# Two-layer encoder on one core: the first weights of the second MLP are made on ACT and POOL while the attention's out-projection still runs, with sums in place and eight operands in borrowed buffers

## The chip, the cores and the metric

One core of a Trainium2 chip. TensorE (PE) multiplies matrices, VectorE (DVE), ScalarE (ACT) and GpSimd (POOL) do elementwise work, SyncE (SP) issues nearly all DMAs. Each engine takes its instructions in the order of its own queue, and semaphores hold an instruction until what it needs is done. The metric is the device time of one execution in microseconds; lower is better. "The clock" is the TensorE clock that the profile says was granted, as a share of full speed.

## The reference

Two residual layers on 1024 tokens of width 1024 (8 tiles of 128 tokens), each a token mixer and a gated MLP. Layer 0 mixes by pooling, layer 1 by differential attention. What matters here is the end of the attention and the MLP behind it:

```python
def _diff_attention(...):
    ...
    return o.reshape(b, s, h * 2 * dh) @ w_o

def _conv_ffn(x, w_up, conv_w, conv_b, w_down):
    g, u = jnp.split(x @ w_up, 2, axis=-1)
    ...                       # gc = conv_b + three-tap convolution of g along the tokens
    act = jax.nn.gelu(gc.astype(jnp.float32), approximate=False).astype(x.dtype)
    return (act * u) @ w_down

# in reference(), per layer i
        h = h + y
        h = h + _conv_ffn(_rms_norm(h, ffn_norm[i]), ffn_w_up[i], ffn_conv_w[i], ffn_conv_b[i], ffn_w_down[i])
```

## The kernel before

**Numbers in two parts.** A float32 operand is held as hi + lo, two fp32r tiles: ACT copies the source into hi (a CAST), and DVE or POOL subtracts hi from the source into lo. A product is three matmuls, hi·hi, hi·lo, lo·hi.

**The MLP's up-projection** runs in 22 units j of 128 columns of u and 128 of g. A unit is a 2 by 2 block product done with seven products instead of eight: its weights are four blocks u1, u2, g1, g2 (512 contraction rows each) and three running sums of them; the tokens are seven activation operands x[1] to x[7], made once for all units. Each product is 12 matmuls of 512 columns, so a unit is 84 matmuls. `load` (L382) fetches a unit's two 512 KB raw weight tiles ru and rg, `prep` (L397) makes its seven operand pairs with `parts` (L391: cast on ACT, subtraction on POOL or DVE), `unit` (L499) issues the products in the order 1, 6, 2, 7, 5, 4, 3. Pairs are in the pool `wc`, which has 16 buffers; `prep` of unit 0 of a layer makes its sums into tiles of the pool `s` and does all but two of its subtractions on DVE (L404).

**The stretch around the change** is the entry to the second MLP. The four last head pairs of the out-projection matrix take all 16 buffers of `wc` (`wo_l`, L1385). `wo_rest` (L1394) runs over the token tiles in the order 0, 4, 1, 5, 2, 6, 3, 7: 24 matmuls into two accumulators `wo_acc`; then `add_halves` (L171) adds the residual on DVE and squares on ACT, `rstd` (L179) makes the scale `rn_v`, and `norm_to_x` (L301) scales the tile into `xs` on ACT (L306), transposes it on PE into `tp` (L313, eight transposes) and reads that out (L323 on DVE, L345 on ACT). `each_with_lag` (L366) emits a tile's `combine` after the next tile's first part: for tiles 0 to 3 it only splits the two halves (x[1] and x[2], in `hnT_hi` and `hnT_lo` of half 0); for tiles 4 to 7 it makes the four sums of the block scheme with the partner tile (L354, L355, L356 and L358, all DVE, SBUF operands) and splits x[3] and x[5] (`hnT` of half 1) and x[4], x[6], x[7] (`x_hi`, `x_lo`), with lo on DVE for two and on POOL for three (L318, L319). After the third tile (`early`, L1405) the MLP generator is started: it emits `load(0)` and, of `prep(0)`, the pairs for products 1 and 2 and the first two sums with the pair for product 6. The rest comes after `load(1)` at the end of the stretch (L731).

The queues of this stretch are ordered by a scheduler from the order of emission, priorities and its own costs; from unit 1 on, PE, DVE and ACT keep the order of emission (L736). Pools `cm` and `wd` have one buffer each, of 8 KB per partition, and no compute instruction touches them through unit 0: `w_combos` of unit 1 (L450) loads 1 MB into `wd` on SP, which is issued at 1286 us, among the loads at the start of the out-projection, and lies there until four DVE sums at L456 to L462 take it from 1463.68 us; `cm` is used from unit 2 by `m_combos` (L467). The functions below have the line numbers of the profile.

Of the kernel before, what the change touches and what calls it, by code (L numbers as in the profile page):

```python
# [12 lines left out]
F32R = mybir.dt.float32r  # L13
I32 = mybir.dt.int32
AF = mybir.ActivationFunctionType
ALU = mybir.AluOpType
# [4 lines left out]
P = 128  # L21
# [3 lines left out]
NF = DFF // P  # L25
NT = S // P
NK = D // P
ORDER = (0, 4, 1, 5, 2, 6, 3, 7)
PLAN = ("...saq.bS..c.p", "st.aS.m.q.fb....F.c..")
PLAN7 = (".as.b....S.pqc.", "tmsaSqcb..f......F..")  # L30
# [59 lines left out]
def trunk_kernel(  # L90
# [36 lines left out]
    def f32(ap):  # L127
        return ap.bitcast(F32)
# [18 lines left out]

    hnT = [[hp.tile([P, NK, 512], F32R, name=f"hnT_{n}{hf}") for n in ("hi", "lo")] for hf in range(2)]
    h_dram = [[dram.tile([P, D], F32, name=f"h_dram{i}_{t}") for t in range(NT)] for i in range(4)]
# [82 lines left out]

    gcol = cp.tile([P, 4, NK], F32, name="gcol")
    neglam = cp.tile([P, 1], F32, name="neglam")
# [66 lines left out]
    def norm_to_x(layer, tt, ar, h_t, ss):  # L301
# [19 lines left out]
        def gained(q, dst):  # L321
            gk = gcol[:, 2 + layer, 4 * q:4 * q + 4].unsqueeze(2).broadcast_to([P, 4, P])
            V.tensor_tensor(dst, pts[q], gk, ALU.mult)  # L323
            return dst

        q0, q1 = slice(0, 4), slice(4, 8)
        if tt < 4:
            xf = ar.xf[tt] = ar.tile("raw", [P, NK, P], F32, "xf")
            gained(0, xf[:, q0])
# [36 lines left out]
    def each_with_lag(tiles, first, early=None):  # L366
        late = None
        for tt in tiles:
            nxt = first(tt)
            if late is not None:  # L370
                late()
            late = nxt
            if tt == 1 and early is not None:
                early()
        late()

    def ffn(layer, ar, tail, extra=None):
        G = nc.gpsimd
        wup, wdn, cv = w_up[layer], w_down[layer], convp[layer]
        raws, ws = {}, {}  # L380

        def load(j):  # L382
            if j >= NF:
                return
            raws.setdefault(j, [])
            for off in (DFF, 0):
                r = ar.tile("g" if layer == j == 0 else "raw", [P, NK, P], F32, "raw")
                nc.sync.dma_start(r, wup[:, off + j * P:off + (j + 1) * P].rearrange("(k p) f -> p k f", p=P))
                raws[j].append(r)

        def parts(src, eng=G):  # L391
            hi, lo = (ar.tile("wc", [P, 4, P], F32R, n) for n in ("w_hi", "w_lo"))
            A.copy(hi, src)  # L393
            eng.tensor_tensor(lo, src, f32(hi), ALU.subtract)  # L394
            return hi, lo

        def prep(j):  # L397
            if j >= NF:
                return
            w = ws.setdefault(j, {})  # L400
            ru, rg = raws.pop(j)
            u1, u2, g1, g2 = ru[:, 0:4], ru[:, 4:8], rg[:, 0:4], rg[:, 4:8]

            eng = (V, G)[j > 0]  # L404

            def s_tile(a, b, op):
                t = ar.tile("s", [P, 2, 512], F32, "s")[:, 0].rearrange("p (k f) -> p k f", f=P)
                eng.tensor_tensor(t, a, b, op)  # L408
                return t

            w[1] = parts(u1, G)
            if j == 0:
                w[2] = parts(u2, G)
            yield
            s1 = s_tile(g1, g2, ALU.add)
            s2 = s_tile(s1, u1, ALU.subtract)
            w[6] = parts(s2, eng)
            yield
            if j:
                w[2] = parts(u2)  # L420
            yield
            w[7] = parts(s_tile(u1, g1, ALU.subtract), eng)
            yield
            w[5] = parts(s1, eng)
            yield
            w[4] = parts(g2, eng)
            yield
            w[3] = parts(s_tile(u2, s2, ALU.subtract), eng)
            yield
# [293 lines left out]
            return ends[2:]  # L723

        load(0)
        first = prep(0)
        next(first)
        if layer:
            next(first)
        yield  # L730
        load(1)  # L731
        for _ in first:
# [17 lines left out]
    ar = Arena("a")  # L750
# [123 lines left out]
    def tail0(tt, r):  # L874
        return norm_to_hnT(ar.h[tt], tt, ar, r)

    mlp = ffn(0, ar, tail0, lambda: before_attention())
    pool_band(0)

# [149 lines left out]
    def proj_qk(j, hf):  # L1029
# [5 lines left out]
        for h in range(2):  # L1035
            acc = ps_pj.tile([P, 512], F32, name="pj")
            n = 0
            for k in range(NK):
                whi, wlo = w_qk[j][k // 2]
                for l, r in ((whi, xhi), (wlo, xhi), (whi, xlo)):  # L1040
                    PE.matmul(acc, l[:, k % 2, h], r[:, k], start=(n == 0), stop=(n == 3 * NK - 1))  # L1041
                    n += 1
# [201 lines left out]
    ar = Arena("b")  # L1244
# [83 lines left out]
    with tc.manual_schedule(engines={mybir.EngineType.PE}):  # L1328
        for g in range(H * NT + 2):
            j, i = divmod(g, NT)  # L1330
# [53 lines left out]
    for j in range(4, 8):  # L1384
        hi, lo = ([ar.tile("wc", [P, 512], F32R, "wo_l") for _ in range(2)] for _ in range(2))  # L1385
        r = ar.tile("raw", [P, D], F32, "rawo")
        nc.sync.dma_start(r, w_o[0][j * P:(j + 1) * P, :])
        for n in range(2):
            A.mul(hi[n], halves(r)[n], subsc)
            V.scalar_tensor_tensor(lo[n], halves(r)[n], subsc, f32(hi[n]), ALU.mult, ALU.subtract)  # L1390
        grp.append((j, hi, lo))
    mlp = ffn(1, ar, lambda *a: tail1(*a), lambda: final_gain())

    def wo_rest(tt):  # L1394
# [9 lines left out]

    each_with_lag(ORDER, wo_rest, lambda: next(mlp))  # L1405

# [55 lines left out]
```

## Time and profile before

| | us |
|---|---|
| three timed runs: median (lowest to highest) | 2075.48 (2073.23 to 2075.9) |
| the profiled execution's own time | 2074.96 |
| its span in the trace | 2073.2 |
| so outside the span | 1.76 |
| mean granted TensorE clock | 0.986 |

The profile's page gives busy time by engine and the chain that ended last; the view of windows gives the same for a stretch, with its granted clock; the view of waits says who waited for whom; the timeline lists instructions with start and duration in us and, in brackets, the idle time ahead of one and what ended it. The stretch of the change is 1360 to 1460 us of the span.

### The profile page before, as it was taken

Reading aid. Unit: us, or ns where it says so; the run is one execution under the profiler, and the core shown is the slowest. Engines: PE = TensorE matmul, PEld = TensorE weight load, DVE = VectorE, ACT = ScalarE, POOL = GpSimd, SP = SyncE. Lnnn points to the kernel's source line nnn. Section 1 sums busy time; section 2 is a strip of 40 time slices with the busy share of each in tenths; the row PEclk is TensorE's granted clock in tenths of the full one; section 3 lists DMA queues with packets and bytes.
Section 4 is the critical chain, followed back from the end, with each engine's and each line's share of the span. In section 5 each row is a group of like instructions: output and inputs, shape, how many; then the busy total and the mean of one; then the engine's idle time right before and its main releaser. Section 6 shows DMA issues by size and latency. Waiting matters only on the chain.

```text
span 2073.2 us, 27646 instructions
## 1 busy us (share of the span) xinstructions
PE 1999.2 (96%) x9659; PEld 1664.9 (80%) x9659; DVE 1553.3 (75%) x2286; ACT 1023.5 (49%) x1838; POOL 891.7 (43%) x676
## 2 busy tenths in 40 slices
PE   6799999999999999999999998998999999999998
PEld 6678888888888877888888887876888888888886
DVE  7867777777675658999889987767766777775665
ACT  7733333333453646666667666565433333344343
POOL 4499999996000000101110111115999999930000
PEclk9899999999999999999999999998999999999999
DMA  4325464453976522122212115253445445458663
GB/s 172 104 90 174 138 192 143 157 173 128 378 227 209 193 67 67 43 70 65 64 44 75 56 42 188 102 191 114 128 142 192 148 158 175 140 197 334 200 212 133
DMA packets 221720, 301.90 MB, mean 146 GB/s; under 512 B 17852, under 2 KB 142092, under 8 KB 218764
## 3 DMA queue, kind: packets, MB, share of 16 engines
q1 hardware_dynamic: 221580, 300.13, 44.4%
q8 instruction: 76, 1.25, 0.3%
q14 instruction: 64, 0.52, 0.1%
HBM read 196.78 MB, written 90.70 MB: 139 GB/s over the span
## 4 chain that ended last, share of the span: by engine, by line
PE 87%; DVE 6%; ACT 2%; DMA 2%; issue 1%; SPq 1%; DVEq 0%; ACTq 0%
PE dn L610 19%; PE up_b L436 17%; PE up_c L436 11%; PE up_a L436 11%; PE pj L1041 7%; PE sc L1127 5%; PE pj L1083 4%; PE po L1169 3%; PE aT L1158 3%; PE pj L1265 2%; PE pp L862 1%; DVE nm L1129 1%; PE pl L842 1%; PE wo_acc L1265 1%; DMA kf<-t 1%
## 5 line engine op out<-in xcount | busy, mean ns | idle before, releaser
L1109 POOL TENSOR_TENSOR q_lo<-qt,q_hi 128x256 fp32r<-128x256 f32 x64 | 49.6, 776 | 680.5 <-ACT q_hi L1108 626.7
L394 POOL TENSOR_TENSOR w_lo<-s,w_hi 128x512 fp32r<-128x512 f32 x168 | 270.6, 1610 | 19.4 <-ACT w_hi L393 19.1
L610 PE MATMUL dn<-hnT_hi 128*128 128x512 f32 x560 | 218.1, 389 | 0.0
L610 PE MATMUL dn<-hnT_hi,hnT_lo 128*128 128x512 f32 x560 | 217.9, 389 | 0.0
L610 PE MATMUL dn<-hnT_lo,hnT_hi 128*128 128x512 f32 x560 | 217.9, 389 | 0.0
L436 PE MATMUL up_b<-x_hi,w_hi 128*128 128x512 f32 x528 | 207.2, 393 | 5.2 <-ACT x_hi L318 4.4
L436 PE MATMUL up_b<-x_lo,w_hi 128*128 128x512 f32 x528 | 207.2, 392 | 1.7 <-DVE x_lo L319 1.7
L394 POOL TENSOR_TENSOR w_lo<-raw,w_hi 128x512 fp32r<-128x512 f32 x130 | 193.7, 1491 | 30.8 <-ACT w_hi L393 29.6
L436 PE MATMUL up_b<-x_hi,w_lo 128*128 128x512 f32 x528 | 206.5, 391 | 0.0
L393 ACT CAST w_hi<-s 128x512 fp32r<-128x512 f32 x176 | 108.7, 618 | 178.7 <-PE up_b L436 90.0
L1129 DVE TENSOR_REDUCE nm<-sc 128x1 f32<-128x1024 f32 x128 | 155.8, 1217 | 15.1 <-PE sc L1127 14.7
L593 ACT CAST hnT_hi<-mst 128x1024 fp32r<-128x1024 f32 (+1 forms) x76 | 74.7, 983 | 167.2 <-PE dn L610 127.5
L594 DVE TENSOR_TENSOR hnT_lo<-mst,hnT_hi 128x1024 fp32r<-128x1024 f32 (+1 forms) x76 | 86.5, 1138 | 92.0 <-ACT hnT_hi L593 91.9
L1132 ACT ACTIVATE prob<-sc,nm 128x1024 f32<-128x1024 f32 x128 | 142.7, 1115 | 23.8 <-DVE nm L1129 11.4
L436 PE MATMUL up_a<-hnT_hi,w_hi 128*128 128x512 f32 x352 | 138.9, 395 | 5.3 <-ACT g L513 4.7
L436 PE MATMUL up_a<-hnT_lo,w_hi 128*128 128x512 f32 x352 | 138.6, 394 | 0.1
L436 PE MATMUL up_a<-hnT_hi,w_lo 128*128 128x512 f32 x352 | 138.2, 393 | 0.0
L408 POOL TENSOR_TENSOR s<-raw 128x512 f32<-128x512 f32 x84 | 133.2, 1586 | 11.4 <-DMA raw<-in_ffn_w_up_dram 4.1
L436 PE MATMUL up_c<-hnT_hi,w_hi 128*128 128x512 f32 x352 | 137.2, 390 | 0.0
L436 PE MATMUL up_c<-hnT_lo,w_hi 128*128 128x512 f32 x352 | 136.9, 389 | 0.0
L436 PE MATMUL up_c<-hnT_hi,w_lo 128*128 128x512 f32 x352 | 136.9, 389 | 0.0
L393 ACT CAST w_hi<-raw 128x512 fp32r<-128x512 f32 x132 | 81.6, 618 | 84.8 <-PE up_c L436 80.6
(317 smaller groups left out, 5447.6 us busy)
## 6 DMA issues: line engine op xcount, KB each, us to landing
raw<-in_ffn_w_up_dram SPq DMA_DIRECT2D x88, 512.0 KB, 4.4
mst<-m_dram SPq DMA_DIRECT2D x70, 512.0 KB, 5.9
wd<-in_ffn_w_down_dram SPq DMA_DIRECT2D x22, 1024.0 KB, 6.0
wd_dram<-wd SPq DMA_DIRECT2D x22, 1024.0 KB, 6.5
m_dram<-cm SPq DMA_DIRECT2D x80, 256.0 KB, 5.6
wst<-wd_dram SPq DMA_DIRECT2D x40, 512.0 KB, 5.2
m_dram<-gc SPq DMA_DIRECT2D x66, 256.0 KB, 6.4
wst<-in_ffn_w_down_dram SPq DMA_DIRECT2D x30, 512.0 KB, 5.5
```

The source lines that it names most:

```text
L393: A.copy(hi, src)
L394: eng.tensor_tensor(lo, src, f32(hi), ALU.subtract)
L408: eng.tensor_tensor(t, a, b, op)
L436: PE.matmul(acc, l[a][:, k], r[b][:, k], start=first and n == 0, stop=n == 11, skip_group_check=True)
L593: A.copy(h_, x)
L594: V.tensor_tensor(l_, x, f32(h_), ALU.subtract)
L610: PE.matmul(banks[t], l[:, q, cols], r[:, q], start=first and cnt == 0, stop=stop and cnt == 3 * n - 1, skip_group_check=True)
L1041: PE.matmul(acc, l[:, k % 2, h], r[:, k], start=(n == 0), stop=(n == 3 * NK - 1))
L1083: PE.matmul(acc, l[:, k % 4], r[:, k], start=(n == 0), stop=(n == 3 * NK - 1))
L1127: PE.matmul(sc[:, ns_], l[:, c], ks[:, c, ns_], start=(l is qhi), stop=(l is qlo))
L1129: V.tensor_reduce(nm, sc, AX.X, ALU.max, negate=True)
L1132: A.activation(soft[j, i][c], sc, AF.Exp, bias=nm, accum_out=sm[:, c, i:i + 1])
```

## The change

For layer 1 alone (`AHEAD_OF_UP`), `prep(0)` gives way to `prep_first`, and the whole of it is emitted at the early point, after the third token tile, ahead of `load(1)`.

```diff
+AHEAD_OF_UP = (1,)
...
+        def two_pairs(where):
+            t = ar.tile(where, [P, 2, 2, 4, P], F32R, "w_hl")
+            return [(t[:, i, 0], t[:, i, 1]) for i in range(2)]
+
-        def parts(src, eng=G):
-            hi, lo = (ar.tile("wc", [P, 4, P], F32R, n) for n in ("w_hi", "w_lo"))
+        def parts(src, eng=G, into=None):
+            hi, lo = into or [ar.tile("wc", [P, 4, P], F32R, n) for n in ("w_hi", "w_lo")]
             A.copy(hi, src)
             eng.tensor_tensor(lo, src, f32(hi), ALU.subtract)
             return hi, lo
+
+        def prep_first():
+            w = ws.setdefault(0, {})
+            ru, rg = raws.pop(0)
+            u1, u2, g1, g2 = ru[:, 0:4], ru[:, 4:8], rg[:, 0:4], rg[:, 4:8]
+            room = dict(zip((7, 5, 4, 3), two_pairs("cm") + two_pairs("wd")))
+            w[1] = parts(u1)
+            w[2] = parts(u2)
+            yield
+            w[4] = parts(g2, G, room[4])
+            G.tensor_tensor(g2, g1, g2, ALU.add)
+            G.tensor_tensor(g1, u1, g1, ALU.subtract)
+            G.tensor_tensor(u1, g2, u1, ALU.subtract)
+            w[6] = parts(u1)
+            w[7] = parts(g1, G, room[7])
+            w[5] = parts(g2, G, room[5])
+            G.tensor_tensor(u2, u2, u1, ALU.subtract)
+            w[3] = parts(u2, G, room[3])
...
-        first = prep(0)
+        first = prep_first() if layer in AHEAD_OF_UP else prep(0)
         next(first)
         if layer:
-            next(first)
+            next(first, None)
```

The pairs for products 7, 5, 4 and 3 are now in `cm` and `wd` (named `w_hl`), those for 1, 2 and 6 stay in `wc`. The four sums overwrite the raw tiles and are done on POOL, as are all seven subtractions. Before, POOL did two of these eleven and DVE nine. The 1 MB load of `wd` for unit 1, which stood among the loads at the start of the out-projection on SP, now stands behind the raw loads of units 1 to 3 and waits for the last matmul of unit 0, which reads `wd`.

On PE the eight transposes of token tile 2 now stand behind three more matmuls of the out-projection than before, those of tile 6 behind four fewer. The scheduler's order changes at two places of the stretch on which the prediction rests. **ACT, at the `xs` of token tile 2** (the fifth in the order). Names: `b` and `t` are the block sums of tile 5, `rn_y` the root in the scale, `w_hl` a weight's hi part in the borrowed buffers. Before:

```order
L345 ACTIVATE b_13747<-tp,gcol 128x128
L193 ACTIVATE rn_y<-ss,rn_b 128x1
L318 CAST hnT_hi_69<-b_13748 128x4x128
L176 ACTIVATE wo_acc,ss<-hs 128x512
L318 CAST x_hi<-t_13818 128x4x128
L306 ACTIVATE xs<-hs,rn_v 128x1024
```

Now:

```order
L346 ACTIVATE b_13757<-tp,gcol 128x128 x4
L319 CAST hnT_hi_69<-b_13758 128x4x128
L398 CAST w_hl<-raw 128x512
L319 CAST x_hi<-t_13828 128x4x128
L177 ACTIVATE wo_acc,ss<-hs 128x512
L319 CAST hnT_hi_69<-b_13757 128x4x128
L194 ACTIVATE rn_y<-ss,rn_b 128x1
L398 CAST w_hl<-raw 128x512 x2
L319 CAST x_hi<-xf 128x4x128 x2
L177 ACTIVATE wo_acc,ss<-hs 128x512
L307 ACTIVATE xs<-hs,rn_v 128x1024
```

Three casts of weights and three more casts of activations (one of `hnT_hi`, two of `x_hi`) now stand ahead of the `xs`, and the last two `w_hl` casts read what POOL's first two sums write. **POOL at the same place**, from tile 5's `hnT_lo` on. Before:

```order
L319 TENSOR_TENSOR hnT_lo_70<-b_13748,hnT_hi_69 128x4x128
L319 TENSOR_TENSOR x_lo<-t_13818,x_hi 128x4x128
L319 TENSOR_TENSOR x_lo<-xf,x_hi 128x4x128
L319 TENSOR_TENSOR hnT_lo_68<-xf,hnT_hi_67 128x4x128
L394 TENSOR_TENSOR w_lo<-raw,w_hi 128x512 x2
```

Now:

```order
L320 TENSOR_TENSOR hnT_lo_70<-b_13758,hnT_hi_69 128x4x128
L399 TENSOR_TENSOR w_hl<-raw,w_hl 128x512
L320 TENSOR_TENSOR x_lo<-t_13828,x_hi 128x4x128
L411 TENSOR_TENSOR raw<-raw 128x512
L412 TENSOR_TENSOR raw<-raw 128x512
L399 TENSOR_TENSOR w_hl<-raw,w_hl 128x512 x2
L320 TENSOR_TENSOR x_lo<-xf,x_hi 128x4x128
```

The second sum (L412) is the fifth instruction from here, and it needs the four ahead of it done. **ACT at the `xs` of token tile 3** (the seventh in the order; `b` and `t` are tile 6's). Before:

```order
L393 CAST w_hi<-raw 128x512
L176 ACTIVATE wo_acc,ss<-hs 128x512
L393 CAST w_hi<-s 128x512
L193 ACTIVATE rn_y<-ss,rn_b 128x1
L318 CAST x_hi<-t_13961 128x4x128
L318 CAST x_hi<-xf 128x4x128
L318 CAST hnT_hi_69<-b_13890 128x4x128
L318 CAST hnT_hi_69<-b_13891 128x4x128
L306 ACTIVATE xs<-hs,rn_v 128x1024
```

Now:

```order
L398 CAST w_hi<-raw 128x512
L177 ACTIVATE wo_acc,ss<-hs 128x512
L398 CAST w_hi<-raw 128x512
L194 ACTIVATE rn_y<-ss,rn_b 128x1
L398 CAST w_hi<-raw 128x512
L319 CAST x_hi<-xf 128x4x128
L398 CAST w_hl<-raw 128x512
L319 CAST x_hi<-t_13971 128x4x128
L307 ACTIVATE xs<-hs,rn_v 128x1024
```

Here too the third `w_hi` cast and the `w_hl` cast read what POOL writes. **POOL at this place**, from tile 6's `hnT_lo` on, now:

```order
L320 TENSOR_TENSOR hnT_lo_70<-b_13901,hnT_hi_69 128x4x128
L399 TENSOR_TENSOR w_lo<-raw,w_hi 128x512
L413 TENSOR_TENSOR raw<-raw 128x512
L399 TENSOR_TENSOR w_lo<-raw,w_hi 128x512
L417 TENSOR_TENSOR raw<-raw 128x512
L399 TENSOR_TENSOR w_lo<-raw,w_hi 128x512
```

The sum that the `w_hl` cast reads (L417) is again the fifth. In the rows of before the two `w_lo` came ahead of tile 6's `hnT_lo`, and no sum was on POOL.

## The prediction

> **What bounds the kernel now.** I read the profile's page first. PE is busy nearly all of the span, and the chain that ended last runs on PE for 87%.
>
> ```profile
> PE 1999.2 (96%) x9659; PEld 1664.9 (80%) x9659; DVE 1553.3 (75%) x2286; ACT 1023.5 (49%) x1838; POOL 891.7 (43%) x676
> PE 87%; DVE 6%; ACT 2%; DMA 2%; issue 1%; SPq 1%; DVEq 0%; ACTq 0%
> ```
>
> So a change is worth what it adds to or takes from PE's idle time and PE's clock. The change touches 1395 to 1460 us; there I asked for windows of 10 us (span, busy time and count of PE, PEld, DVE, ACT and POOL, PE's granted clock, DMA share, GB/s).
>
> ```profile
> 1400.00:1410.00 10.00, 10.00 (x49) 8.17 (x48) 9.43 (x19) 6.77 (x15) 3.74 (x3) 1.00 0.61 224
> 1410.00:1420.00 10.00, 8.64 (x42) 6.62 (x40) 8.52 (x16) 6.90 (x16) 7.01 (x5) 1.00 0.20 82
> 1420.00:1430.00 10.00, 5.50 (x16) 4.02 (x17) 7.72 (x19) 7.08 (x13) 5.07 (x4) 0.62 0.24 67
> 1430.00:1440.00 10.00, 7.24 (x28) 5.24 (x27) 6.99 (x8) 5.53 (x12) 3.47 (x3) 0.84 0.09 38
> ```
>
> PE loses time from 1410 to 1440 and its clock falls to 0.62 and 0.84 there, while DVE, ACT and POOL are each busy 35 to 85%: latency, not throughput. The waits of PE from 1360 to 1480 us say for what:
>
> ```profile
> PE tp L313 <- ACT xs L306: 6.6, 3, 3.9
> PE up_b L436 <- DVE x_lo L319: 1.3, 1, 1.3
> PE up_b L436 <- ACT x_hi L318: 0.8, 1, 0.8
> PE up_b L436 <- DVE u L524: 0.8, 1, 0.8
> PE up_a L436 <- ACT g L513: 0.7, 1, 0.7
> PE up_a L436 <- ACT hnT_hi L318: 0.6, 1, 0.6
> ```
>
> No row names a weight of unit 0: `w_hi` and `w_lo` come early enough as it is. The change can help only by freeing DVE, and can hurt by holding ACT's `xs`, for which PE waits most. PE's timeline gives the tiles and the clock (the transposes of tiles 5, 2, 6, 3, then matmuls; their columns are start, duration, in brackets the idle time ahead and its releaser):
>
> ```profile
> 1398.15 1.03 PE L313 MATMUL tp<-ident,xs 128*128 128x128 f32 x8
> 1406.17 1.09 PE L313 MATMUL tp<-ident,xs 128*128 128x128 f32 x8
> 1413.53 1.09 PE L313 MATMUL tp<-ident,xs 128*128 128x128 f32 x8 [1.24 <-ACT xs L306]
> 1423.79 1.97 PE L313 MATMUL tp<-ident,xs 128*128 128x128 f32 x8 [3.91 <-ACT xs L306]
> 1428.28 0.63 PE L436 MATMUL up_a<-hnT_hi,w_hi 128*128 128x512 f32 x1
> 1428.70 0.63 PE L436 MATMUL up_a<-hnT_lo,w_hi 128*128 128x512 f32 x1
> 1432.40 0.57 PE L436 MATMUL up_a<-hnT_hi,w_hi 128*128 128x512 f32 x1
> 1434.67 0.39 PE L436 MATMUL up_a<-hnT_hi,w_lo 128*128 128x512 f32 x1
> 1434.90 0.39 PE L436 MATMUL up_a<-hnT_hi,w_hi 128*128 128x512 f32 x1
> 1439.70 0.79 PE L436 MATMUL up_b<-x_lo,w_hi 128*128 128x512 f32 x1 [1.28 <-DVE x_lo L319]
> 1454.68 0.39 PE L436 MATMUL up_a<-hnT_hi,w_hi 128*128 128x512 f32 x1
> ```
>
> After the 3.91 us of idle time the transposes take 1.97 for 1.09, and matmuls start 0.42 us apart, where 0.23 is usual; that lasts to 1432.40, 8.6 us. After 1.24 alone it does not begin; after 1.28, the last of several short waits, it does for a while (0.79 for 0.39). The last row is unit 1's first matmul.
>
> **The change part by part.** Prices first: timelines of ACT (`xs`, the square in two records, a pair of casts), DVE and POOL.
>
> ```profile
> 1398.85 0.88 ACT L345 ACTIVATE b<-tp,gcol 128x128 f32<-128x128 f32 x3 [0.30 <-PE tp L313]
> 1404.97 1.15 ACT L306 ACTIVATE xs<-hs,rn_v 128x1024 f32<-128x1024 f32 x1
> 1408.44 0.60 ACT L176 ACTIVATE wo_acc<-hs 128x512 f32<-128x512 f32 x1
> 1421.54 1.13 ACT L318 CAST hnT_hi<-b 128x512 fp32r<-128x512 f32 x2
> 1422.58 1.15 ACT L306 ACTIVATE xs<-hs,rn_v 128x1024 f32<-128x1024 f32 x1
> ```
> ```profile
> 1400.54 0.69 DVE L408 TENSOR_TENSOR s<-raw 128x512 f32<-128x512 f32 x1 [1.74 <-DMA raw<-in_ffn_w_up_dram]
> 1403.73 0.68 DVE L354 TENSOR_TENSOR t<-b,b 128x512 f32<-128x512 f32 x1
> 1404.80 1.32 DVE L355 TENSOR_TENSOR b<-b,xf 128x512 f32<-128x512 f32 x1
> 1406.15 1.66 DVE L356 TENSOR_TENSOR xf<-t,xf 128x512 f32<-128x512 f32 x1
> 1436.68 1.76 DVE L408 TENSOR_TENSOR s<-raw 128x512 f32<-128x512 f32 x1
> 1440.17 1.77 DVE L394 TENSOR_TENSOR w_lo<-s,w_hi 128x512 fp32r<-128x512 f32 x1
> ```
> ```profile
> 1403.76 1.80 POOL L319 TENSOR_TENSOR hnT_lo<-b,hnT_hi 128x512 fp32r<-128x512 f32 x1 [5.89 <-ACT hnT_hi L318]
> 1405.52 1.74 POOL L319 TENSOR_TENSOR x_lo<-t,x_hi 128x512 fp32r<-128x512 f32 x1
> 1450.47 1.28 POOL L408 TENSOR_TENSOR s<-raw,s 128x512 f32<-128x512 f32 x1
> ```
>
> A POOL operation of 128x512 takes 1.28 us alone and 1.74 to 1.80 beside DVE's sums; a DVE sum takes 0.68 alone and 1.32 to 1.66 beside POOL's. So each operation moved from DVE to POOL takes about twice as long, and slows what DVE keeps. The Trainium skill ("SBUF — State Buffer", section "Who interferes with whom") calls the port pair that VectorE and GpSimd share an exclusive lock. The trace agrees: both sides are longer by about one operation of the other. That rule speaks against this change.
>
> *First hold: tile 2's `xs`.* In the new order ACT must first cast two `w_hl` that POOL's first two sums write, and the second sum is the fifth POOL operation counted from tile 5's `hnT_lo`. Tile 5's transposes, 1398.15 + 1.03, don't move. ACT reads out four blocks of 0.29, from 1398.85 to 1400.0, and casts in 0.6: POOL starts at about 1400.7. The raw tile lands at 1400.54 (the row of L408), so nothing is earlier. Five operations are 6.4 us at 1.28 and 8.8 at 1.76; DVE is busy 9.43 of 10 us there, mostly with sums, so I take 8.4: 1409.1. Then the last `w_hl` cast (0.51, half of the 1.13 pair less its overlap), two `x_hi` (1.0), a square (0.6) and `xs` (1.15): 1412.4. PE is at these transposes at 1406.17 plus three matmuls of 0.23, or 1406.9. In before it did not wait there. **New stall: 5.5 us** (bounds 3.5 and 5.9 by the two POOL prices).
>
> *Clock behind it.* An idle time of 5.5 is longer than the 3.91 that halved the clock. At the same price, transposes lose 0.9 and fifteen matmuls 0.2 each in 8.6 us: **+3.9** (bounds 0, if the 3.91 was not the cause, and 3.9). The Trainium skill ("TensorE: Matmul & The Clock Gate", section "What's actually happening") has the clock halved after an idle window of about 3.4 us. By it the lower bound of 3.5 would still do it.
>
> *Tile 6's 1.24* goes: its `xs` is made while PE runs late: **−1.2**. The out-projection up to tile 6's transposes is then 5.5 + 3.9 − 1.2 = 8.2 us later. These transposes now stand four matmuls (0.9) earlier in PE's order, so they end at about 1413.53 + 8.2 − 0.9 + 1.09 = 1421.9.
>
> *Second hold: tile 3's `xs`.* The same again: a `w_hl` cast that reads the fifth POOL operation from tile 6's `hnT_lo` on. Readout and cast take 1.3 as before, so POOL starts at 1423.2, ends five at 8.2 us (1.64 each, since DVE is less busy) at 1431.4; cast, `x_hi` and `xs` are 2.2: 1433.6, against 1423.79. The transposes of tile 3 come 9.8 us later, of which 8.2 are told: the 3.91 stall becomes 5.5, **+1.6** (bounds −0.2 at 1.28, +2.2 at 1.76). The half clock behind it is there in before as well and adds nothing.
>
> *From tile 3's transposes to unit 1*, 30.9 us in before. DVE loses a sum and a subtraction of 1.76 and 1.77, a gain for the 1.3 that PE waits for `x_lo`. But POOL's operations for unit 1's weights, now ahead of the last tile's `hnT_lo` and `x_lo` in its queue, fall beside DVE's last block sums, at about 1 us more for each (1.66 for 0.68), and some four of these stand between the last transposes and the last `x_lo`. Net **+1.3** (bounds 0, where the gain pays for it, and 3).
>
> *Late load.* `wd` is now loaded only after unit 0.
>
> ```profile
> wd<-in_ffn_w_down_dram SPq DMA_DIRECT2D x22, 1024.0 KB, 6.0
> 1463.68 1.16 DVE L456 TENSOR_TENSOR wd<-wd 128x512 f32<-128x512 f32 x1
> ```
>
> Its 6.0 us begin with unit 1, and DVE reached its sum 9.0 us after that start in before (1463.68 less 1454.68): hidden by 3 us, **0** taken. If the load takes over 9 us (it shares queues with raw loads), DVE's later readouts of unit 1 queue behind the sum, and PE behind these.
>
> *Unit 1's weights* are ready earlier, but no wait of PE asks for them: 0. Less work on DVE in the rest of the kernel: 0, since only unit 0 changes.
>
> The sum is 5.5 + 3.9 − 1.2 + 1.6 + 1.3 = **+11.1**. The profiled execution took 2074.96 us; with 11.1 it is 2086.1, and I give 2086.0. The median of the timed runs is 0.52 above the profiled one, which I leave inside the range.
>
> **The rivals.**
>
> *Faster: DVE's relief decides.* DVE loses nine operations, among them two sums at 1400.5 and 1401.8 just where tile 5's block sums queue. Were tile 2's `xs` not held, tile 6's block sums and so tile 3's `xs` would come earlier, and the 3.91 with its half clock (3.9) would shrink: 2074.96 less 5 to 8, about 2068. The point that decides: POOL's second sum is done by 1404.0, one cast ahead of the `xs` that ran at 1404.97. From 1400.7 POOL would have 3.3 us for five operations, and even at 1.28 they are 6.4. Chance 0.07.
>
> *No change: the first stall is taken back.* If the second hold did not happen and tile 3's `xs` came with its old distance to the transposes of tile 6 less DVE's relief, the 3.91 would shrink by what DVE sheds there, about 4 us of sums and subtractions, and its clock loss would only move ahead: about 2076. Against it: the fifth POOL operation stands there in the order too. Chance 0.06.
>
> *The stalls without the clock.* The clock loss is not paid twice, by a shorter stall or because the phase behind tile 2's stall overlaps the second one: 11.1 − 3.9 = 7.2, 2082. For it: 0.62 is a mean over 10 us, and one event is thin evidence for a rule. Chance 0.27; it is on the forecast's side.
>
> *The load is late.* It lands after 9 us, and PE waits up to 3 us in unit 1: 2089. Against it: median 6.0. Chance 0.12.
>
> The forecast itself has 0.48.
>
> **How the numbers follow.** The low terms (3.5 + 0 − 1.2 − 0.2 + 0) give +2.1, but all low at once is unlikely; with POOL at 1.28 in one hold and the clock loss at zero it is about +4, or 2079. The high terms (5.9 + 3.9 − 1.2 + 2.2 + 3) give +13.8, with the late load over that; 2090 leaves out only their far end. The range 2079.0 to 2090.0 holds the forecast and its two neighbours for most of their 0.87, and leaves out the faster and the no-change case. A run of this kernel tells about 0.2%, 4 us, from no change: below 2071.3 is faster, 0.07; the no-change case and a little of the stalls' low end are the same, 0.08; the rest is slower, 0.85.
>
> **What would show it right or wrong.** In the waits of PE, `tp <- ACT xs` should grow from 6.6 us to 11 or more, with one stall of about 5.5 ahead of tile 2's transposes, where none was, and none ahead of tile 6's. ACT's idle time ahead of the second `w_hl` cast should name POOL's sum (L412), and five POOL operations should stand back to back from 1400.7. The granted clock should fall in the window from 1410 to 1420, where it was 1.00. Unit 1's first matmul should start near 1466. If tile 2's transposes start by 1408, the step on POOL's queue is wrong; if the stall is there and the clock stays, the clock term; if unit 1 starts near 1466 but the end comes later still, the `wd` load.

## The result, and the profile after

The changed kernel took 2087.07 us (median of four runs, 2084.76 to 2088.24), the kernel before 2075.19 in the runs beside them: a ratio of 1.0059, 95% interval 1.0048 to 1.0071, so 11.9 us slower. Forecast were 2086.0 and slower.

The page of the profiled execution (2088.24 us, the longest of the four) gives every engine the same share of the span as before. One number stands out: DVE has nine operations fewer (2277 for 2286) and is busy 12.5 us longer.

```profile
span 2086.5 us, 27639 instructions
PE 2002.9 (96%) x9659; PEld 1668.1 (80%) x9659; DVE 1565.8 (75%) x2277; ACT 1023.2 (49%) x1838; POOL 898.5 (43%) x685
```

The windows over the stretch (columns as before) place it. PE is idle for 4 to 5 us in the windows from 1410 and from 1430 (before: in the one from 1420). The clock is below 1.00 in four of the five windows (before: in three, at 0.62, 0.84 and 0.86). POOL is busy 64 to 100% from 1410 on, where it was 35 to 70% up to 1450 before.

```profile
1410.00:1420.00 10.00, 5.67 (x23) 4.97 (x24) 6.66 (x16) 7.34 (x14) 6.35 (x5) 0.83 0.33 107
1420.00:1430.00 10.00, 7.24 (x36) 5.76 (x34) 8.29 (x13) 4.75 (x12) 7.27 (x5) 1.00 0.13 52
1430.00:1440.00 10.00, 5.42 (x15) 4.01 (x16) 4.56 (x11) 7.45 (x14) 7.97 (x7) 0.55 0.72 210
1440.00:1450.00 10.00, 7.27 (x30) 4.71 (x28) 7.70 (x6) 5.14 (x11) 9.47 (x7) 0.94 0.00 0
1450.00:1460.00 10.00, 7.38 (x22) 5.85 (x22) 3.27 (x3) 2.70 (x5) 10.00 (x9) 0.66 0.39 107
```

The waits of PE from 1385 to 1485 us: the wait for `xs` has about doubled, and so have the three below it, for the operands of tile 3 and of the last tile.

```profile
PE tp L314 <- ACT xs L307: 12.7, 3, 6.0
PE up_b L459 <- DVE x_lo L320: 2.6, 1, 2.6
PE up_b L459 <- ACT x_hi L319: 1.7, 1, 1.7
PE up_a L459 <- ACT hnT_hi L319: 1.3, 1, 1.3
```

PE's timeline, the transposes of tiles 1, 5, 2, 6 and 3, two waits behind them, and unit 1's first matmul:

```profile
1395.99 1.09 PE L314 MATMUL tp<-ident,xs 128*128 128x128 f32 x8 [1.46 <-ACT xs L307]
1400.36 1.03 PE L314 MATMUL tp<-ident,xs 128*128 128x128 f32 x8
1414.33 1.97 PE L314 MATMUL tp<-ident,xs 128*128 128x128 f32 x8 [5.20 <-ACT xs L307]
1420.07 1.03 PE L314 MATMUL tp<-ident,xs 128*128 128x128 f32 x8
1433.28 1.97 PE L314 MATMUL tp<-ident,xs 128*128 128x128 f32 x8 [6.04 <-ACT xs L307]
1448.24 0.50 PE L459 MATMUL up_b<-x_hi,w_hi 128*128 128x512 f32 x1 [1.75 <-ACT x_hi L319]
1452.63 0.80 PE L459 MATMUL up_b<-x_lo,w_hi 128*128 128x512 f32 x1 [2.62 <-DVE x_lo L320]
1468.11 0.39 PE L459 MATMUL up_a<-hnT_hi,w_hi 128*128 128x512 f32 x1
```

This execution reaches the stretch 2.2 us later than the profiled one of before (tile 1's transposes at 1395.99 for 1393.78, ahead of every moved instruction); with that taken off, unit 1 starts 11.2 us late. Both stalls stand where they were forecast, and none is left ahead of tile 6.

ACT's timeline shows the queue at tile 2's `xs`, DVE's the scale that it also needs:

```profile
1409.29 0.62 ACT L398 CAST w_hl<-raw 128x512 fp32r<-128x512 f32 x1 [3.68 <-POOL raw L411]
1410.96 0.62 ACT L398 CAST w_hl<-raw 128x512 fp32r<-128x512 f32 x1 [1.05 <-POOL raw L412]
1413.15 1.13 ACT L307 ACTIVATE xs<-hs,rn_v 128x1024 f32<-128x1024 f32 x1
```
```profile
1406.33 0.20 DVE L195 TENSOR_SCALAR rn_v<-ss,rn_c 128x1 f32<-128x1 f32 x1
1406.51 1.60 DVE L359 TENSOR_TENSOR xf<-xf 128x512 f32<-128x512 f32 x1
1408.11 1.70 DVE L320 TENSOR_TENSOR hnT_lo<-b,hnT_hi 128x512 fp32r<-128x512 f32 x1
1410.51 0.20 DVE L198 TENSOR_SCALAR rn_v<-rn_v,rn_y 128x1 f32<-128x1 f32 x1
```

The casts wait for POOL as the prediction said. But the last step of the scale `rn_v` stands on DVE behind sums that take 1.6 to 1.7 us for 0.68, and ends at 1410.71. Without any cast ahead of it, `xs` could have started there, 2.4 us earlier than it did, and would still have been late. So the agreement of the sum does not yet say which cause it was.

DVE's order has changed here too, which neither the rows of order ahead of the prediction nor the prediction itself show. In the kernel before, the last step of this scale ran ahead of the slowed block sums (L355 at 1404.80 and L356 at 1406.15, in the prediction's rows):

```profile
1404.67 0.20 DVE L197 TENSOR_SCALAR rn_v<-rn_v,rn_y 128x1 f32<-128x1 f32 x1
```

Now even its first step (L195) runs behind two of them, L356 and L357, and the others run between slowed operations.

At tile 3's `xs`, the second stall, the scale is ready at 1428.33, and `xs` starts 3.75 us later, behind the casts. There the queue alone holds it:

```profile
1428.13 0.20 DVE L198 TENSOR_SCALAR rn_v<-rn_v,rn_y 128x1 f32<-128x1 f32 x1
```
```profile
1431.04 0.62 ACT L398 CAST w_hl<-raw 128x512 fp32r<-128x512 f32 x1 [2.21 <-POOL raw L417]
1432.08 1.15 ACT L307 ACTIVATE xs<-hs,rn_v 128x1024 f32<-128x1024 f32 x1
```

### The profile page after: what moved, and what is told of

It reads as the page before. It is cut to its first block, busy times and chain, and to the rows that moved or that the text cites. A ratio compares the mean times of both kernels' runs of the same rounds, so it can differ in the third digit from the quotient of the medians.

```text
span 2086.5 us, 27639 instructions
## 1 busy us (share of the span) xinstructions
PE 2002.9 (96%) x9659; PEld 1668.1 (80%) x9659; DVE 1565.8 (75%) x2277; ACT 1023.2 (49%) x1838; POOL 898.5 (43%) x685
## 4 chain that ended last, share of the span: by engine, by line
PE 86%; DVE 6%; ACT 3%; issue 2%; DMA 1%; SPq 1%; POOL 1%; ACTq 0%; DVEq 0%; POOLq 0%
PE dn L633 19%; PE up_b L459 17%; PE up_c L459 11%; PE up_a L459 11%; PE pj L1064 7%; PE sc L1150 5%; PE pj L1106 4%; PE po L1192 3%; PE aT L1181 2%; PE pj L1288 2%; PE wo_acc L1288 1%; PE pp L885 1%; DVE nm L1152 1%; PE pl L865 1%; DMA kf<-t 1%
## 5 line engine op out<-in xcount | busy, mean ns | idle before, releaser
L399 POOL TENSOR_TENSOR w_lo<-s,w_hi 128x512 fp32r<-128x512 f32 x168 | 264.6, 1575 | 23.5 <-ACT w_hi L398 23.1
L1155 ACT ACTIVATE prob<-sc,nm 128x1024 f32<-128x1024 f32 x128 | 142.7, 1115 | 24.8 <-DVE nm L1154 11.9
```

The source lines that it names most:

```text
L1155: A.activation(soft[j, i][c], sc, AF.Exp, bias=nm, accum_out=sm[:, c, i:i + 1])
```

## The theories and the experiments

**Theory A, the queue**: `xs` is held on ACT behind casts that wait for POOL's sums (the prediction's). **Theory B, the port**: POOL's operations make DVE's two-operand operations take 1.7 us for 0.68, and what is made on DVE, the scale included, is late whatever stands on ACT. **Theory C**: the borrowed buffers, by the late load of `wd`; C′: by letting weight work come forward, since it no longer waits for buffers of `wc`. **Theory D**, formed after the second run: unit 1's weights, which now come forward too, meet the last tile's work on POOL and ACT.

For every run I take, in its one profiled execution, the time from tile 0's transposes (the start of the stretch) to those of tile 3, and from there to unit 1's first matmul. Before they took 45.5 and 30.9 us; the table gives what was added. The ratio is to the kernel before, in the runs beside them. Its median there lay between 2072.85 and 2075.19 us, so rows are better compared by their ratios than by their medians.

| run | to tile 3 | from there to unit 1 | median, us | ratio and interval |
|---|---|---|---|---|
| changed kernel | +7.3 | +3.9 | 2087.07 | 1.0059 (1.0048 to 1.0071) |
| e1 casts on POOL | +4.6 | +3.2 | 2082.04 | 1.0041 (1.0029 to 1.0053) |
| e2 all on DVE | −1.6 | +8.4 | 2082.45 | 1.0041 (1.0029 to 1.0054) |
| e3 engine only | +0.4 | +2.7 | 2077.25 | 1.0021 (1.0011 to 1.0031) |
| e4 rest late | +0.1 | +13.0 | 2087.62 | 1.0064 (1.0044 to 1.0084) |
| e5 buffers only | −1.1 | +2.8 | 2076.53 | 1.0015 (1.0005 to 1.0024) |
| e6 unit 1 gated | +7.5 | −2.1 | 2086.90 | 1.0060 (1.0045 to 1.0075) |
| e7 DVE, gated | −1.6 | +0.8 | 2075.43 | 1.0007 (0.9998 to 1.0017) |
| e8 x[7] on DVE | −5.6 | +1.7 | 2072.44 | 0.9986 (0.9975 to 0.9997) |
| e9 x[7], x[3] on DVE | −6.0 | +0.4 | 2070.94 | 0.9983 (0.9974 to 0.9992) |
| e10 no POOL | −3.9 | −1.8 | 2071.64 | 0.9987 (0.9979 to 0.9996) |
| e11 operands on DVE | +2.3 | +5.2 | 2081.85 | 1.0041 (1.0027 to 1.0056) |
| e12 wd on ACT | +8.5 | −1.5 | 2079.70 | 1.0035 (1.0022 to 1.0048) |

### e1: the casts off ACT

```diff
-        def parts(src, eng=G, into=None):
+        def parts(src, eng=G, into=None, cast=A.copy):
...
-            A.copy(hi, src)
+            cast(hi, src)
...
-            w[6] = parts(u1)
-            w[7] = parts(g1, G, room[7])
-            w[5] = parts(g2, G, room[5])
+            w[6] = parts(u1, cast=G.tensor_copy)
+            w[7] = parts(g1, G, room[7], G.tensor_copy)
+            w[5] = parts(g2, G, room[5], G.tensor_copy)
...
-            w[3] = parts(u2, G, room[3])
+            w[3] = parts(u2, G, room[3], G.tensor_copy)
```

> The hi casts of products 6, 7, 5 and 3 are moved from ACT to POOL, so no cast that waits for a POOL sum stands ahead of an xs on ACT; POOL has four operations more. Theory A (queue: the xs is held behind the waiting casts): the stalls ahead of the transposes of tiles 2 and 3 fall from 5.2 and 6.0 us to about 0 and 4, total 2076 to 2079 us. Theory B (shared port: POOL working without a break makes DVE's sums take 1.7 us for 0.68, and the scale rn_v that xs needs is late on DVE): both stalls stay at 3 us or more, total 2082 to 2087 us.

Measured: 2082.04 us, at the lower end of B's range, with stalls of 4.34 and 3.14 us where A had about 0 and 4. Tile 2's `xs` now stands on ACT with no cast of a weight ahead of it that waits, and still comes late. Its row and the scale's:

```profile
1409.40 1.15 ACT L307 ACTIVATE xs<-hs,rn_v 128x1024 f32<-128x1024 f32 x1 [2.86 <-DVE rn_v L198]
```
```profile
1404.29 1.60 DVE L359 TENSOR_TENSOR xf<-xf 128x512 f32<-128x512 f32 x1
1405.88 1.69 DVE L320 TENSOR_TENSOR hnT_lo<-b,hnT_hi 128x512 fp32r<-128x512 f32 x1
1407.68 1.56 DVE L320 TENSOR_TENSOR x_lo<-xf,x_hi 128x512 fp32r<-128x512 f32 x1
1409.16 0.20 DVE L198 TENSOR_SCALAR rn_v<-rn_v,rn_y 128x1 f32<-128x1 f32 x1
```

The hold on ACT is real but worth 2.7 of the 7.3 us up to tile 3 (with four operations more on POOL, so perhaps more). Most of that is the second stall, which falls from 6.04 to 3.14 us; the first falls from 5.20 to 4.34. The other 4.6 are there without it, and tile 2's `xs` waits for DVE alone. A is not enough; B is seen at work, though the run has DVE's new order as well as its slower operations, and doesn't part the two.

### e2: the same order, with DVE in POOL's place

The four sums and five subtractions of `prep_first` get `V` for `G`:

```diff
-            w[4] = parts(g2, G, room[4])
-            G.tensor_tensor(g2, g1, g2, ALU.add)
+            w[4] = parts(g2, V, room[4])
+            V.tensor_tensor(g2, g1, g2, ALU.add)
...
```

> The changed kernel with its buffers, its in-place sums and its early emission, but the four sums and five of the subtractions back on DVE. Theories A and B: the cost goes with POOL, total 2075 to 2079 us. Theory C (the cost comes from the borrowed buffers and the late load of wd): total stays at 2085 to 2088 us.

Measured: 2082.45, in neither range. Up to tile 3 A and B are right: that part is 1.6 us shorter than before. DVE here also makes sums between the steps of tile 2's scale, but mostly at 0.68 us, and the last step ends at 1406.82:

```profile
1406.62 0.20 DVE L198 TENSOR_SCALAR rn_v<-rn_v,rn_y 128x1 f32<-128x1 f32 x1
```

With the offsets at tile 5's transposes taken off, that is 1406.5, against 1408.5 in the changed kernel and 1404.9 before. So the price and the order of DVE's operations both seem to count.

But behind tile 3 8.4 us are lost, more than in the changed kernel. Two waits hold most of it (PE, from 1385 to 1440 us):

```profile
PE up_a L459 <- ACT hnT_hi L319: 4.8, 1, 4.8
PE up_b L459 <- ACT x_hi L319: 4.3, 1, 4.3
```
```profile
1428.61 0.62 ACT L319 CAST hnT_hi<-xf 128x512 fp32r<-128x512 f32 x1 [0.83 <-DVE xf L324]
1436.33 0.62 ACT L398 CAST w_hi<-s 128x512 fp32r<-128x512 f32 x1 [2.44 <-POOL s L431]
1438.56 0.62 ACT L319 CAST x_hi<-xf 128x512 fp32r<-128x512 f32 x1 [0.57 <-DVE xf L357]
```

The first wait ends with the cast at 1428.61, which waits for tile 3's readout on DVE; that stands behind tile 6's sums. The second ends with the cast at 1438.56, which waits for the last tile's sum L357 on DVE. Of DVE's six operations for the last tile four take 1.57 to 1.84 us here, beside work for unit 1's weights on POOL; in e7, where that work is held back, the same four take 0.68 or 0.69. On ACT too a cast for these weights waits among the last tile's (1436.33). This led to theory D.

### e3, e4, e5: one part at a time

e3 is the kernel before with the engine alone changed, e4 the changed kernel without the second early step, e5 the kernel before with the four pairs in the borrowed buffers.

```diff
e3
-            eng = (V, G)[j > 0]
+            eng = (V, G)[j > 0 or layer > 0]
e4
-        if layer:
-            next(first, None)
e5
+            room = dict(zip((7, 5, 4, 3), two_pairs("cm") + two_pairs("wd"))) if layer and j == 0 else {}
...
-            w[5] = parts(s1, eng)
+            w[5] = parts(s1, eng, room.get(5))
```

> The kernel before with only the engine changed: unit 0's sums and subtractions in the second MLP on POOL, buffers and emission as before. On ACT one cast that reads a POOL sum stands ahead of the xs of tile 3, none ahead of that of tile 2. Theory A: no more than one short hold, total 2075 to 2078 us. Theory B: DVE is slowed wherever POOL works, total 2080 us or more.

Measured: 2077.25 us, 3.1 us more in the stretch, nearly all of it in the last part. That is in A's range and below B's; but the kernel before was at 2072.85 beside it, and 4.4 us more than that lies between the two.

> The changed kernel, but only the pairs of products 1 and 2 are emitted early, the rest after the out-projection. On ACT the two waiting casts stay ahead of tile 2's xs, and tile 3's xs now stands ahead of the casts that waited there. Theory A: the first stall stays at about 5 us, the second goes from 6.0 to 1 us or less, total 2080 to 2083 us. Theory B: the POOL work is only shifted behind, where it meets the last tiles' block sums, total 2085 us or more.

Measured: 2087.62. The stall ahead of tile 3 is gone, as A said, and nothing is won: 13.0 us are lost behind, as B said. POOL's work meets the last two tiles instead: four of DVE's operations from 1426.22 to 1433.02 take 1.62 to 1.76 us each.

> The kernel before with only the pairs of products 7, 5, 4 and 3 in the borrowed buffers; engines, sums and emission as before. Theory C' (the buffers let weight work, unit 0's and unit 1's, come ahead of the last tiles' work, since nothing waits for wc any more): 2 to 6 us slower than before, with the loss between the last transposes and unit 1. Theory A or B alone: no POOL work is added, so within 2 us of before.

Measured: 2076.53, 1.7 us more in the stretch, with the loss in the last part: C′ is right at its lower edge. On POOL the first operation for unit 1's weights starts at 1438.99, where before it was 1445.46, so unit 1's weights did come forward. No single part carries the cost: engine 3.1, buffers 1.7, and together with the early emission and the sums in place 11.2.

### e6, e7: unit 1's weights held back

```diff
             gained(1, b22)
+            ar.gate = b22
...
+                if layer and j == 1:
+                    V.tensor_copy(r[:, 0, 0:1], ar.gate[:, 0, 0:1])
                 nc.sync.dma_start(r, wup[:, off + j * P:off + (j + 1) * P].rearrange("(k p) f -> p k f", p=P))
```

> The changed kernel, but the loads of unit 1's weights wait for the readout of the last tile, by a copy of one column that DVE makes into the raw tiles first, so no POOL operation of unit 1 can stand ahead of the last tile's. Theory D (the loss behind tile 3's transposes, 3.9 us in the changed kernel, comes from unit 1's sums on POOL beside the last block sums): the stalls for x_hi and x_lo fall from 4.4 to about 2 us and unit 1 starts 3 to 4 us earlier in the stretch; total 2083 to 2084 us if unit 1 then finds its weights ready, 2087 if it has to wait for them. Theory B without D (unit 0's POOL work is all): nothing moves, 2087 us.

> As the kernel with all on DVE, which lost 6.8 us in the stretch, and with the loads of unit 1 gated in the same way. Theory D: what was left there was unit 1's work on POOL; the stretch comes back to about that of before, total 2074 to 2078 us. Otherwise it stays at 2081 to 2083 us.

e7 is e2 with the same gate, and came to 2075.43: its last part lost 0.8 us for 8.4, so 7.6 us of e2's loss came with unit 1's weights. (Its wait for `hnT_hi` stays, 5.7 us: PE is there sooner, and tile 3's readout stands behind tile 6's sums on DVE.) In e6 the waits for `x_hi` and `x_lo` fell from 4.4 to 1.2 us and unit 1 started 5.8 us earlier in the stretch; the last part is then 2.1 us shorter than before, where unit 0's sums still stood among DVE's last ones (L408 at 1436.68 in the prediction's rows). D holds in both. But e6's total did not move. Three waits of PE from 1440 to 1560 us, and DVE's timeline:

```profile
PE up_b L462 <- DVE g L557: 4.1, 1, 4.1
PE up_b L462 <- ACT x_hi L319: 0.7, 1, 0.7
PE up_b L462 <- DVE x_lo L320: 0.5, 1, 0.5
```
```profile
1473.86 1.66 DVE L482 TENSOR_TENSOR wd<-wd 128x512 f32<-128x512 f32 x1 [5.90 <-DMA wd<-in_ffn_w_down_dram]
1475.55 1.64 DVE L484 TENSOR_TENSOR wd<-wd 128x512 f32<-128x512 f32 x1
1477.11 0.68 DVE L557 TENSOR_TENSOR g<-up_b,g 128x512 f32<-128x512 f32 x1
```

This is the prediction's rival of the late load, made real by the gate: on SP the load of `wd` now stood behind raw loads that waited, was issued at 1467.30, 7.4 us after unit 1's start, and DVE stood before its sum with the readout `g` queued behind it.

### e12: the load of wd on another queue

```diff
-            nc.sync.dma_start(t, w_pair(q))
+            (nc.scalar if layer and not (q or started) else nc.sync).dma_start(t, w_pair(q))
```

> The changed kernel with unit 1's loads gated as in the run before, and the first load of wd issued from ACT's queue, so that it no longer stands behind the raw loads on SP. The wait of 4.1 us for it in unit 1 goes: total 2081 to 2084 us. If unit 1's weights are late as well: 2085 us or more.

Measured: 2079.70, below the range given, though the interval of its ratio reaches into it (2079 to 2084 us). The ratio is 1.0035 against e6's 1.0060, which is 5.2 us. The wait of 4.1 us is gone; what stays is the loss up to tile 3, 8.5 us in this execution. So the two halves of the loss are separate: weights of unit 0 beside tiles 2 to 3, and weights of unit 1 beside tile 7. (The gate is in this run as well.)

### e8, e9, e10, e11: work taken off POOL

If POOL is what costs, the kernel before should gain from less of it. e8 moves x[7]'s subtraction to DVE, e9 also x[3]'s, e10 all of the operands' and those of the weights of products 1 and 2; e11 does it for the operands of the changed kernel.

```diff
e8
-                put(7, t3, G)
+                put(7, t3, V if layer else G)
```

> The kernel before with one subtraction per tile (x[7] lo of the second MLP) moved the other way, from POOL to DVE. Theory B: POOL is idle where DVE makes the other block sums, these take 0.7 us for 1.3 to 1.7, the scale of tile 3 is ready sooner, and its stall of 3.9 us shrinks: total 2070 to 2073 us, less than before. Theory A alone: DVE has more to do, 2075 to 2077 us.

> The kernel before with two subtractions per tile (x[7] lo and x[3] lo of the second MLP) on DVE. Theory B: again less POOL work beside the block sums, tile 3's stall gone, total 2069 to 2072 us. Rival (DVE becomes the bound): the readouts queue on DVE, total 2074 us or more.

> The kernel before with every subtraction of the last tiles and of the weights of products 1 and 2 on DVE, so that POOL does nothing in the stretch until unit 1's weights. Theory B in its strong form (only the shared port counts): at least as fast as with one subtraction moved, 2069 to 2072 us. Rival (DVE becomes the bound): slower than with one or two moved, 2074 us or more.

> The changed kernel with all subtractions of the activation operands on DVE, so that POOL has weights alone and its queue starts on them earlier. Theory A and B together: the sums are done sooner and the stalls ahead of tiles 2 and 3 shrink, total 2080 to 2083 us. If the last stretch alone counted: 2086 to 2088 us.

Measured: 2072.44, 2070.94, 2071.64 and 2081.85. The first three are faster than the kernel before, and e9 beats both kernels (0.9983, interval 0.9974 to 0.9992). In e10 POOL does nothing in the stretch until unit 1's weights, DVE does everything, and it is still faster than before: DVE had the room. e11 falls to B's and A's common range. One group of DVE's, the block sum of line 356 (357 after), from 1395 to 1455 us, in the kernel before, the changed one, and e9 (count, busy time, mean ns, idle time):

```profile
L356 DVE TENSOR_TENSOR xf<-t,xf 128x512 f32<-128x512 f32 x3 | 5.0, 1652 | 0.1
```
```profile
L357 DVE TENSOR_TENSOR xf<-t,xf 128x512 f32<-128x512 f32 x3 | 5.0, 1659 | 0.1
```
```profile
L356 DVE TENSOR_TENSOR xf<-t,xf 128x512 f32<-128x512 f32 x3 | 2.1, 685 | 0.0
```

The sum of before was already paying for POOL in all three tiles; e9 made it 0.97 us shorter each time. The Trainium skill ("SBUF — State Buffer", section "Who interferes with whom") has the port pair as an exclusive lock, and "Perfetto Trace Analysis", section "Optimizing Scalar/DVE Operations", warns that moving work between those two engines may not help. These runs agree: 685 ns alone, 1659 beside POOL, which is longer by about three quarters of a POOL operation's 1.28 us, and no run that moved DVE's work to POOL gained.

## Why the prediction came out right, and where its steps were wrong

In the stretch 11.1 us were forecast and 11.2 measured, and the signs named beforehand were there: the waits for `xs` at 12.7 us, the clock at 0.83 from 1410, unit 1 at 1465.9 less the offset. But two terms were off by 2.4 and 2.6 us, and their errors cancelled; that the sum is right to 0.1 us is luck.

- *First stall*: forecast 5.5, measured 5.20. POOL started its five operations at 1400.65 (less the 2.2 offset) for 1400.7 and ended at 1408.7 for 1409.1; PE arrived at 1406.9 as said. The price of the queue was right, and in this kernel the queue is what ended last. But it was not the only cause: the prediction took the scale as ready and did not look at DVE's order, and e1 shows `xs` waiting 2.86 us for the scale with the queue out of the way, with 4.34 of the 5.20 us left.
- *Clock behind it*: forecast 3.9, measured 1.5 (from tile 2's to tile 6's transposes 5.74 us, of which eight transposes are 0.85 and fifteen matmuls 3.4 at full speed). The clock did halve (transposes 1.97 us), but only for 3.0 us; by 1417.34 matmuls were 0.23 us apart again. This term was taken from one earlier event of 8.6 us, and was mis-sized; behind the second stall the half speed lasted 8.6 again (1433.28 to 1441.84).
- *Tile 6's stall* went, as said.
- *Second stall*: 6.04 for 5.5, held by the queue as said, with the scale ready; tile 3's transposes came 7.3 us late for 9.8, nearly all of the difference being the clock term.
- *From tile 3 to unit 1*: forecast +1.3, measured +3.9. This is the step that failed: it priced POOL's work for unit 1 at some four DVE operations slowed by 1 us, less DVE's gain, and had no clock loss. By e6 the gain is 2.1 us (the part is that much shorter than before without unit 1's work), and unit 1's work cost 6.0 (3.9 + 2.1).

  The two traces show where the 6.0 went. DVE's six operations of the last tile, from its first block sum to the end of the last `x_lo`, take 9.66 us in the changed kernel and 6.00 in e6, so 3.7 more, near the four of 1 us. PE's waits are longer by 3.5. Behind the last of them, the 2.62 us for `x_lo`, the clock halves: thirteen matmuls on PE take 5.7 us from there, and 3.1 behind e6's wait of 0.47. These 2.6 us had no place in the term. The first and the last of the six on DVE, in the changed kernel and in e6, then PE's rows:

```profile
1442.92 1.18 DVE L355 TENSOR_TENSOR t<-b,b 128x512 f32<-128x512 f32 x1
1450.83 1.75 DVE L320 TENSOR_TENSOR x_lo<-xf,x_hi 128x512 fp32r<-128x512 f32 x1
```
```profile
1440.79 0.69 DVE L356 TENSOR_TENSOR t<-b,b 128x512 f32<-128x512 f32 x1
1446.11 0.68 DVE L320 TENSOR_TENSOR x_lo<-xf,x_hi 128x512 fp32r<-128x512 f32 x1
```
```profile
1458.31 0.63 PE L459 MATMUL up_c<-hnT_hi,w_hl 128*128 128x512 f32 x2
```
```profile
1446.85 0.50 PE L462 MATMUL up_b<-x_lo,w_hi 128*128 128x512 f32 x1 [0.47 <-DVE x_lo L320]
1449.94 0.61 PE L462 MATMUL up_c<-hnT_hi,w_hl 128*128 128x512 f32 x2
```

- *Late load*: 0 forecast and seen. DVE reached its sum 8.8 us after unit 1's start, and the load had taken 4.9. That it decides where it is issued late, behind raw loads that wait, is what e6 shows.
- *The rival on the faster side* needed POOL's second sum by 1404.0; it ended at 1408.7 (less the offset). The rival of no change lost by the second stall. The one without the clock was nearer on that term than the forecast (1.5 lies nearer to 0 than to 3.9) and lost on the sum.

Not settled: how the engine (3.1), the buffers (1.7) and the early emission with sums in place add up to 11.2; each also changes the scheduler's order for the others, and emission alone with the other two as before was not run. Nor did a run part DVE's new order from its slower operations at tile 2's scale.

## What to carry to other kernels

POOL was busy for only 43% of the span, but a POOL operation beside DVE's two-operand ones takes its time from DVE: read the mean duration of the same DVE group in a stretch with and without POOL before moving work there, and try the other direction too. When a small work item is brought forward, look at what the freed buffers let come forward with it; here the next unit's weights cost 6.0 us, nearly as much as the 7.3 us up to tile 3 that came with the moved work. When a sum agrees with the measurement, check each term against the trace: here two errors of some 2.5 us hid each other. And price the clock behind every stall that a change makes longer, not only behind the first.

## What was unexpected of the hardware

The half clock is not a matter of the stall's length alone. In e2 and e7 PE stalls for the same 2.29 us ahead of tile 3's transposes, and these take 1.97 us in the one and 1.09 in the other:

```profile
1422.52 1.97 PE L314 MATMUL tp<-ident,xs 128*128 128x128 f32 x8 [2.29 <-ACT xs L307]
```
```profile
1421.81 1.09 PE L314 MATMUL tp<-ident,xs 128*128 128x128 f32 x8 [2.29 <-ACT xs L307]
```

In e1 a stall of 3.14 us leaves them at 1.11. The Trainium skill ("TensorE: Matmul & The Clock Gate", section "What's actually happening") puts the threshold at about one window of 3.4 us idle; a stall of 2.29 was enough once here, and one of 3.14 was not at first. Where in such a window a stall falls might decide, but no run here tests it.
